# A decoder layer in split fp32: the place of one weight cast at the start and of one product at the end

## The chip, the cores and the metric

The kernel runs on one core of a Trainium2 chip. A core has a matrix engine (PE, which loads its stationary operand through PEld), a vector engine (DVE), a scalar engine (ACT), GpSimd (POOL) and SyncE (SP), which issues most of the DMAs. Every engine works through a queue of its own, in order, and waits for the others by semaphores. The metric is the device time of one execution in microseconds; lower is better. The time before is 980.24 us, the median of three runs (980.25, 978.34 and 980.24).

## What is computed

The input x has 1024 rows (positions) and 1024 columns. The reference, cut to what matters here:

```python
h = rms_norm(x, pre_g)                      # rows scaled by 1/root(mean of squares), columns by pre_g
z = jnp.einsum('bsd,de->bse', h, w_in)      # 1024 x 1024 by 1024 x 7184
qa, ka, va, ga, qb, kb, vb, gb, gk_low = split_columns(z)
oa = diff_attention(qa, ka, va, lam)        # 8 heads; then a norm and a gate silu(ga)
ob = gla_chunked(qb, kb, vb, log_a)         # 4 heads of gated linear attention; norm, gate silu(gb)
y = jnp.einsum('bse,ed->bsd', jnp.concatenate([oa, ob], axis=-1), w_out)
return x + rms_norm(y, post_g)
```

The change touches the first two lines of this and the last one. [...]

## The kernel before, in words

**The input product.** z is worked out by a scheme of seven block products instead of eight (Strassen's). h is cut into four blocks h11, h12, h21, h22 of 512 rows by 512 columns, each kept transposed, and each pair of weight column groups into four blocks b11 to b22. A list `order` of pairs (p, n) says which of the products n = 1 to 7 of which weight group p comes next; it begins (0,1), (1,1), (0,2), (1,2). Groups 0 and 1 belong together ("wide"), so they share their weights: (0,1) and (1,1) use the cast of b11, (0,2) and (1,2) that of b21. The **third product** of the title is (0,2), the first that needs b21 and h12. `prepare(i)` calls `make_weights(i)` (L278), which casts the weights of product i on ACT (L315, hi) and subtracts on DVE (L316, lo). For the first four products the cast is queued with `issue_after` behind two instructions of the last row norm: an Exp on ACT (L1481) and a `tensor_scalar` on DVE (L1482). `issue_after` orders the queue of the engine that the named instruction is on, and adds no wait.

**The beginning.** Eight tiles of x, 128 rows each, are loaded, with the first weights behind the first four. `norm_x(st)` (L486) for tiles 0 to 3 takes the sum of squares on ACT (L491), the root through `rstd` (L1477: Ln and Exp on ACT, a correction step on DVE) and scales half of the columns on DVE, the other half on POOL (L482). `first(0)` (L529) transposes the scaled tiles on PE into four PSUM banks called xT (L120), one for every 128 columns; `put` (L519) makes h_hi of each on ACT (L521) and h_lo on DVE (L522), and POOL adds the two to f1hi (L542). These four pairs are h11. Product (0,1) follows, called x in the trace; then `first(1)` does the same for h12, and (1,1) and (0,2) follow. `norm_x` of tiles 4 and 5 and of 6 and 7 (called xt in the trace) comes behind that in the program; POOL scales these whole (L482), and `blocks(j)` transposes them from 30 us on.

**What sets the order.** The program's text is no schedule: a scheduler at build time simulates the engines and fixes the order of each queue, by readiness and by the place in the text. Matmuls and transposes keep the order of the text (L116, L119). `pin` (L977) with a true first argument, and `keep_in_program_order`, fix an instruction behind the one before it in the text on the same engine. Where nothing is pinned, ACT's and DVE's orders come from the simulation.

**The end.** The output product is accumulated in PSUM for eight row tiles, in the order ENDS. `finish(n)` (L1436) does the last matmuls of tile n (called yps in the trace), squares each half of 512 columns on ACT with a running sum (L1445; its second part, ACTIVATION_READ_ACCUMULATOR, delivers the sum), takes the root with `rstd` and multiplies by post_g and the root. For the last two tiles (LAST = 2) the product with post_g is made by itself, so that only one instruction for each half (L1464, which also adds x) is left behind the root: half 0 in L1451, half 1 in L1455, which is queued behind `rstd`'s first DVE instruction, the sum for the root (L1482).

Of the kernel before, what the change touches and what calls it, by code (L numbers as in the profile page):

```python
# [10 lines left out]
AF = mybir.ActivationFunctionType  # L11
ALU = mybir.AluOpType
# [5 lines left out]
NT = S // P  # L18
KT = D // P
HB = 4  # L20
# [11 lines left out]
def hymba_kernel(  # L32
# [20 lines left out]
    nc = tc.nc  # L53
    act, dve, pool, pe, sp = nc.scalar, nc.vector, nc.gpsimd, nc.tensor, nc.sync

    def fp(t):
        return t.bitcast(F32)

    def cols(half):
        return slice(half * 512, half * 512 + 512)  # L60
# [3 lines left out]
    pre_g = const.tile([P, KT], F32, name="pre_g")  # L64
# [45 lines left out]
    def take_bank(shape, name):  # L110
        i = free.pop(0)
        return bank(i, shape, name), i
# [6 lines left out]
    def tr(dst, src):  # L119
        tc.keep_in_program_order(pe.transpose(dst, src, ident))  # L120
# [25 lines left out]
    def at(part, j):  # L146
        per = HB // len(part)
        return part[j // per][:, j % per]
# [53 lines left out]
    y, z = len(pairs) - 2, len(pairs) - 1  # L202
# [35 lines left out]
    def prepare(i):  # L238

        if i >= len(order) or i in ws:  # L240
            return
        if i < 4:

            act_ins, dve_ins = normed[0][:2]
            with tc.issue_after(act_ins.ins), tc.issue_after(dve_ins.ins):
                make_weights(i)
        else:
            make_weights(i)
# [29 lines left out]
    def make_weights(i):  # L278
        p, n = order[i]
        if wide(p) and p % 2:  # L280
            ws[i] = ws_wide[p - 1, n]
            return
        if p in early and n < 3:
            src = early[p][n - 1]
        else:
            fetch_raw(p, n, i)
            if wide(p):
                (b11, b21), (b12, b22) = ([raws[q].get(kh) for kh in range(2)] for q in (p, p + 1))
            else:
                top, bot = raws[p][0], raws[p][1]  # L290
                b11, b12 = top[:, :, :P], top[:, :, P:]
                b21, b22 = bot[:, :, :P], bot[:, :, P:]


            def sub(dst, a, b):
                dve.tensor_tensor(dst, a, b, ALU.subtract)  # L296
                return dst

            if n == 5:
                src = sub(b11, b12, b11)  # L300
            elif n == 6:
                src = sub(b11, b22, b11)
            elif n == 4:
                src = sub(b21, b21, b11)
            elif n == 7:
                src = sub(b12, b22, b12)
            else:
                src = {1: b11, 2: b21, 3: b22}[n]
        if wide(p):
            w = [ap.tile([P, HB, 256], F32R, tag="ring", name="w", bufs=NRING) for _ in range(2)]  # L310
            ws_wide[p, n] = w
        else:
            w2 = ap.tile([P, 2, HB, P], F32R, tag="ring", name="w", bufs=NRING)
            w = [w2[:, 0], w2[:, 1]]
        act.copy(w[0], src)  # L315
        dve.tensor_tensor(w[1], src, fp(w[0]), ALU.subtract)  # L316
        ws[i] = w
# [163 lines left out]
        x_cs = xs[st][:, cs]  # L481
        return engine.tensor_scalar(x_cs, x_cs, norms[st], 1.0, ALU.mult, ALU.mult)  # L482

    norms, normed = {}, []

    def norm_x(*sts):  # L486
        n = len(sts)
# [30 lines left out]

    def put(ps, k, dst, j):  # L519
        hi, lo = dst  # L520
        act.activation(at(hi, j), ps, AF.Copy, scale=pre_g[:, k : k + 1])  # L521
        dve.scalar_tensor_tensor(  # L522
            at(lo, j), ps, pre_g[:, k : k + 1], fp(at(hi, j)), ALU.mult, ALU.subtract
        )


# [2 lines left out]
    def first(h):  # L529

        ps = [take_bank([P, 512], "xT") for _ in range(HB)]
        for i in range(4):
            for j in range(HB):
                k = h * HB + j
                tr(ps[j][0][:, i * P : (i + 1) * P], xs[i][:, k * P : (k + 1) * P])
        hi, lo = H[("h11", "h12")[h]]
        for j in range(HB):
            put(ps[j][0], h * HB + j, (hi, lo), j)
            if h:
                act.activation(f1[h][:, j], ps[j][0], AF.Copy, scale=pre_g[:, h * HB + j : h * HB + j + 1])  # L540
            else:
                pool.tensor_tensor(f1[h][:, j], fp(at(hi, j)), fp(at(lo, j)), ALU.add)  # L542
            free.append(ps[j][1])

    def parts(n, j, f):
        hi, lo = block(n)
        act.copy(at(hi, j), f)
        dve.tensor_tensor(at(lo, j), f, fp(at(hi, j)), ALU.subtract)  # L548
# [46 lines left out]
    def go(n):  # L595
        for _ in range(n):
            i = made[0]
            if i == len(order):
                return
            made[0] = i + 1  # L600
            for a in range(4):
                prepare(i + a)
            step(i)
            if order[i][0] > EARLY and not (wide(order[i][0]) and order[i][0] % 2):
                wo_step(order[i][1])
            if fill and next(fill[0], 0) == 0:
                fill.pop(0)

    prepare(0)
    first(0)  # L610
    for i in range(1, 4):
        prepare(i)
    go(1)
    first(1)
    go(2)
    norm_x(4, 5)
# [360 lines left out]
    def pin(first, ins):  # L977

        if first:
            tc.keep_in_program_order(ins)  # L980
# [385 lines left out]
    parts_d, ps_d = {}, {}  # L1366
    opened.update(dict.fromkeys(Y))

    LAST, ENDS = 2, [4, 5, 6, 7, 0, 1, 2, 3]
# [12 lines left out]
    def last_times(st, dh, part, e):  # L1382
        mh, ml = part
        hi, lo = wo[e]
        for i, (a, b) in enumerate(((mh, hi), (ml, hi), (mh, lo))):
            mm(
                ps_d[st, dh], a[:, e - 4, :], b[:, cols(dh)],
                start=False, stop=(e == 7 and i == 2), skip_group_check=True,
            )
# [16 lines left out]
    post_g = fin.tile([P, D], F32, name="post_g", bufs=1)  # L1406
# [29 lines left out]
    def finish(n):  # L1436
        st = ENDS[n]
        rows = slice(st * P, (st + 1) * P)
        y = fin.tile([P, D], F32, name="y")
        ssq = const.tile([P, 4, 1], F32, tag="end_ssq", name="ssq", bufs=3)  # L1440
        for dh in range(2):
            for e in range((8, 8, 7 - 3 * dh)[n] if n < 3 else 4, 8):
                last_times(st, dh, parts_d[st], e)
            junk = fin.tile([P, 512], F32, name="junk", bufs=2)
            pin(True, act.activation(  # L1445
                junk, ps_d[st, dh], AF.Square, scale=D**-0.5, accum_out=ssq[:, 2 + dh]
            ))
            if not dh:
                dve.tensor_scalar(ssq[:, 0], ssq[:, 2], EPS, None, ALU.add)
                if n >= NT - LAST:  # L1450
                    dve.tensor_tensor(y[:, cols(0)], ps_d[st, 0], post_g[:, cols(0)], ALU.mult)  # L1451
        ins = rstd(nc, ssq, ssq[:, 3], ssq[:, 0])[2]
        if n >= NT - LAST:
            with tc.issue_after(ins.ins):
                dve.tensor_tensor(y[:, cols(1)], ps_d[st, 1], post_g[:, cols(1)], ALU.mult)  # L1455
        for dh in range(2):
            cs = cols(dh)
            if n < NT - LAST:
                dve.scalar_tensor_tensor(
                    y[:, cs], ps_d[st, dh], ssq[:, 1], post_g[:, cs], ALU.mult, ALU.mult  # L1460
                )
                pool.dma_start(out[0, rows, cs], y[:, cs], accum_op=ALU.add)
            else:
                dve.scalar_tensor_tensor(  # L1464
                    y[:, cs], y[:, cs], ssq[:, 1], xts[n][:, cs], ALU.mult, ALU.add
                )
                sp.dma_start(out[0, rows, cs], y[:, cs])
# [3 lines left out]
    for n in range(NT):  # L1471
        prime(n + 2)
        fetch(n + 4)
        finish(n)


def rstd(nc, t, s, eps, pin=None):  # L1477

    pin = pin or (lambda ins: ins)
    pin(nc.scalar.activation(t[:, 1], s, AF.Ln, bias=eps))  # L1480
    exp = pin(nc.scalar.activation(t[:, 1], t[:, 1], AF.Exp, scale=-0.5))  # L1481
    half = pin(nc.vector.tensor_scalar(t[:, 2], s, eps, -0.5, ALU.add, ALU.mult))  # L1482
    if t.shape[2] == 1:
        pin(nc.vector.scalar_tensor_tensor(
            t[:, 2], t[:, 1], t[:, 2], t[:, 1], ALU.mult, ALU.mult
        ))
    else:
        pin(nc.vector.tensor_tensor(t[:, 2], t[:, 2], t[:, 1], ALU.mult))
        pin(nc.vector.tensor_tensor(t[:, 2], t[:, 2], t[:, 1], ALU.mult))
    last = nc.vector.scalar_tensor_tensor(  # L1490
        t[:, 1], t[:, 2], 1.5, t[:, 1], ALU.add, ALU.mult
    )
    return exp, pin(last), half
# [32 lines left out]
```

## Time and profile before

| | |
|---|---|
| median of three runs | 980.24 us |
| the profiled execution's own time | 979.08 us |
| its span, first to last instruction | 977.4 us |
| time of that execution outside the span | 1.7 us |
| instructions | 15766 |
| mean clock granted to PE | 0.999 |
| PE's three longest waits after its first product | 1.3, 0.9 and 0.7 us |

A row of the timeline reads: start in us from the span's beginning, duration in us, engine, line of the kernel, operation, tile written and tiles read, shapes, and how many instructions were merged; in brackets stands how long the engine was idle before and what ended that. A row of the chain reads: start, duration, engine, tile and line. The chain is followed back from the last instruction to what released each step. Neighbouring instructions of one engine are shown to overlap by about 0.1 us, since the next begins while the last one drains; so the distance of two starts tells what an instruction costs its queue.

### The profile page before, as it was taken

How to read it: one execution, taken by the hardware profiler on the slowest of the kernel's cores; microseconds unless marked ns; L12 is line 12 of the kernel's file. 1: busy time of each engine (PE TensorE's matmuls, PEld its weight loads, DVE VectorE, ACT ScalarE, POOL GpSimd, SP SyncE). 2: the span in 40 equal slices, each digit the busy share in tenths (PEclk: the TensorE clock that was granted, in tenths of full speed). 3: DMA queues.
4: the chain of work that ended last, by engine and by line, in shares of the span. 5: the costliest groups of instructions: out<-in, count | busy, mean ns of one | idle time of the engine just before them, and what ended most of it. 6: DMA issues, size and time to landing. Idle time of an engine off the chain costs nothing.

```text
span 977.4 us, 15766 instructions
## 1 busy us (share of the span) xinstructions
PE 956.7 (98%) x5338; PEld 830.4 (85%) x5338; DVE 735.4 (75%) x1452; ACT 600.5 (61%) x1164; POOL 142.9 (15%) x158
## 2 busy tenths in 40 slices
PE   5999999999999999999999999999999999999997
PEld 5998988888889998999888888878888888888785
DVE  6887597789866667686786876487888888898554
ACT  8742455487357455454665775366776687887773
POOL 4300000000000010000200002121322222443321
PEclk9999999999999999999999999999999999999999
DMA  9432446656774868897987866987656669994677
GB/s 345 151 110 91 139 135 205 231 179 225 238 247 162 264 187 286 254 294 229 293 259 243 273 202 191 407 269 272 197 186 228 240 199 344 340 294 105 151 208 147
DMA packets 152593, 220.45 MB, mean 226 GB/s; under 512 B 17104, under 2 KB 83664, under 8 KB 152416
## 3 DMA queue, kind: packets, MB, share of 16 engines
q1 hardware_dynamic: 146176, 203.71, 64.1%
q0 software_dynamic: 6336, 15.73, 7.0%
q8 instruction: 42, 0.69, 0.3%
q14 instruction: 39, 0.32, 0.1%
HBM read 133.93 MB, written 88.60 MB: 228 GB/s over the span
## 4 chain that ended last, share of the span: by engine, by line
PE 95%; DVE 2%; ACT 1%; DMA 1%; issue 1%; POOL 0%; SPq 0%; DVEq 0%; ACTq 0%; POOLq 0%
PE x L117 24%; PE y L117 15%; PE z L117 15%; PE ypart L117 13%; PE sc L117 7%; PE po L117 5%; PE yps L117 4%; PE wtr L120 3%; PE gpo L117 3%; PE kv L117 1%; PE gkl_ps L117 1%; PE pa L117 1%; DMA x<-in_x_dram 1%; PE xT L120 1%; DVE s_lo L548 0%
## 5 line engine op out<-in xcount | busy, mean ns | idle before, releaser
L315 ACT CAST w<-w_raw 128x512 fp32r<-128x512 f32 (+1 forms) x164 | 112.4, 688 | 94.7 <-PE y L117 44.1
L316 DVE TENSOR_TENSOR w<-w_raw,w 128x512 fp32r<-128x512 f32 (+1 forms) x164 | 126.7, 774 | 50.1 <-ACT w L315 43.3
L1049 ACT ACTIVATE p<-p,stt 128x896 f32<-128x896 f32 (+7 forms) x128 | 99.3, 777 | 36.7 <-DVE stt L1039 33.9
L427 ACT COPY s<-x 128x512 f32<-128x512 f32 x84 | 49.1, 585 | 84.4 <-PE x L117 84.3
L775 POOL TENSOR_SCALAR_AFFINE_SELECT gan<-gan 128x512 f32<-128x512 f32 x8 | 16.5, 2060 | 485.4 <-ACT gan L774 449.8
L296 DVE TENSOR_TENSOR w_raw<-w_raw 128x512 f32<-128x512 f32 (+1 forms) x96 | 75.9, 791 | 13.9 <-DMA w_raw<-in_w_in_dram 12.6
L1039 DVE CUSTOM_DVE_ANT_0 p<-sc,maskt 128x512 f32<-128x512 f32 (+3 forms) x128 | 74.3, 585 | 14.5 <-PE sc L117 13.3
L117 PE MATMUL ypart<-wo_hi,m_hi 128*128 128x512 f32 x192 | 79.5, 414 | 0.1
L117 PE MATMUL y<-h_hi,w 128*128 128x512 f32 x320 | 79.6, 391 | 0.0
L117 PE MATMUL z<-s_hi,w 128*128 128x512 f32 x320 | 79.6, 391 | 0.0
L117 PE MATMUL x<-s_hi,w 128*128 128x512 f32 x320 | 79.6, 391 | 0.0
L1055 POOL TENSOR_SCALAR p<-p,stt,lam 128x1024 f32<-128x1024 f32 (+3 forms) x64 | 56.2, 879 | 146.9 <-DVE stt L1054 141.9
L117 PE MATMUL ypart<-wo_hi,m_lo 128*128 128x512 f32 x192 | 75.5, 393 | 0.0
L117 PE MATMUL ypart<-wo_lo,m_hi 128*128 128x512 f32 x192 | 75.4, 393 | 0.0
L117 PE MATMUL sc<-k,q 128*128 128x512 f32 (+1 forms) x192 | 69.0, 363 | 1.3 <-DVE stt L1039 1.2
L117 PEld LDWEIGHTS x<-s_hi,w 128*128 128x128 f32 x320 | 59.7, 188 | 12.2
L117 PEld LDWEIGHTS y<-h_hi,w 128*128 128x128 f32 x320 | 59.6, 188 | 12.2
L117 PEld LDWEIGHTS z<-s_hi,w 128*128 128x128 f32 x320 | 59.5, 188 | 12.0
L117 PE MATMUL sc<-ks,q 128*128 128x512 f32 (+1 forms) x192 | 66.1, 347 | 0.0
L1097 ACT CAST wt_hi<-wtr 128x512 fp32r<-128x512 f32 (+1 forms) x80 | 42.7, 534 | 24.6 <-PE wtr L120 23.8
L1098 DVE TENSOR_TENSOR wt_lo<-wtr,wt_hi 128x512 fp32r<-128x512 f32 (+1 forms) x80 | 50.7, 633 | 8.6 <-ACT wt_hi L1097 8.0
L1058 DVE SCALAR_TENSOR_TENSOR p<-p,stt,p 128x1024 f32<-128x1024 f32 (+3 forms) x64 | 52.1, 814 | 4.1 <-POOL p L1055 3.9
(226 smaller groups left out, 2247.7 us busy)
## 6 DMA issues: line engine op xcount, KB each, us to landing
w_raw<-in_w_in_dram SPq DMA_DIRECT2D x56, 512.0 KB, 4.7
wo_raw<-in_w_out_dram SPq DMA_DIRECT2D x32, 256.0 KB, 3.0
wo_d<-wo_hi SPq DMA_DIRECT2D x32, 256.0 KB, 2.8
wo_d<-wo_raw SPq DMA_DIRECT2D x32, 256.0 KB, 3.8
q<-q_d SPq DMA_DIRECT2D x32, 256.0 KB, 4.7
k<-k_d SPq DMA_DIRECT2D x32, 256.0 KB, 5.7
ks<-k_d SPq DMA_DIRECT2D x64, 128.0 KB, 6.2
v<-v_d SPq DMA_DIRECT2D x16, 512.0 KB, 7.0
```

What stands on the lines that cost most here:

```text
L117: tc.keep_in_program_order(pe.matmul(*a, **k))
L120: tc.keep_in_program_order(pe.transpose(dst, src, ident))
L296: dve.tensor_tensor(dst, a, b, ALU.subtract)
L315: act.copy(w[0], src)
L316: dve.tensor_tensor(w[1], src, fp(w[0]), ALU.subtract)
L427: act.copy(b[k], ps)
L1039: ins = dve.tensor_tensor_reduce(p[:, a:e], sc[:, : e - a], maskt[:, NZ + P - (e - a) :] if last else maskt[:, : e - a], 1.0, 3e38 if i == ...
L1049: act.activation(p[:, :n], p[:, :n], AF.Exp, bias=st[:, m : m + 1], scale=-1.0, accum_out=st[:, 2 + m : 3 + m],)
L1055: pool.tensor_scalar(p1[:, :n], p1[:, :n], st[:, 5:6], lam, ALU.mult, ALU.mult)
L1058: dve.scalar_tensor_tensor(p0[:, :n], p0[:, :n], st[:, 4:5], p1[:, :n], ALU.mult, ALU.subtract)
L1097: act.copy(hi[:, :n], pt[:, :n])
L1098: dve.tensor_tensor(lo[:, :n], pt[:, :n], fp(hi[:, :n]), ALU.subtract)
```

## The change

It has two parts that do not touch each other.

1. `first` returns the ACT and DVE instructions of its last `put`, and those of `first(0)` are kept in `firsts`. `prepare(1)` to `prepare(3)`, which come behind `first(0)` in the text, queue their weight casts behind these two in place of the norm's two. Of these only `prepare(2)` issues anything: one cast on ACT and one subtraction on DVE of 128x1024 (the odd products (1,1) and (1,2) take over the weights of (0,1) and (0,2)). `prepare(0)` runs while `firsts` is empty and stays where it was. No DMA is issued in it, since both halves of the raw weights are asked for ahead.
2. For the last tile alone (n = 7) the product of half 1 with post_g is pinned behind the earlier DVE instruction of the text, that is ahead of `rstd`, and `rstd`'s five instructions are pinned behind it in the text's order. Tile n = 6 keeps its order.

```diff
-            act_ins, dve_ins = normed[0][:2]
+            act_ins, dve_ins = firsts or normed[0][:2]
             with tc.issue_after(act_ins.ins), tc.issue_after(dve_ins.ins):
                 make_weights(i)
...
-        act.activation(at(hi, j), ps, AF.Copy, scale=pre_g[:, k : k + 1])
-        dve.scalar_tensor_tensor(
-            at(lo, j), ps, pre_g[:, k : k + 1], fp(at(hi, j)), ALU.mult, ALU.subtract
+        return act.activation(at(hi, j), ps, AF.Copy, scale=pre_g[:, k : k + 1]), (
+            dve.scalar_tensor_tensor(
+                at(lo, j), ps, pre_g[:, k : k + 1], fp(at(hi, j)), ALU.mult, ALU.subtract
+            )
         )
...
-            put(ps[j][0], h * HB + j, (hi, lo), j)
+            last = put(ps[j][0], h * HB + j, (hi, lo), j)
...
+        return last
...
     prepare(0)
-    first(0)
+    firsts += first(0)
     for i in range(1, 4):
         prepare(i)
...
-        ins = rstd(nc, ssq, ssq[:, 3], ssq[:, 0])[2]
-        if n >= NT - LAST:
+        if n == NT - 1:
+            pin(True, dve.tensor_tensor(y[:, cols(1)], ps_d[st, 1], post_g[:, cols(1)], ALU.mult))
+        ins = rstd(nc, ssq, ssq[:, 3], ssq[:, 0], lambda ins: pin(n == NT - 1, ins) or ins)[2]
+        if NT - LAST <= n < NT - 1:
             with tc.issue_after(ins.ins):
                 dve.tensor_tensor(y[:, cols(1)], ps_d[st, 1], post_g[:, cols(1)], ALU.mult)
```

More of the change, by code (lines that the diff above doesn't have):

```diff
@@ L482, in scale_x @@
         return engine.tensor_scalar(x_cs, x_cs, norms[st], 1.0, ALU.mult, ALU.mult)
-    norms, normed = {}, []
+    norms, normed, firsts = {}, [], []
     def norm_x(*sts):
```

## The prediction

> **What bounds the kernel now.** I read the page's busy shares and its chain first, then the waits of PE from the first product on, then the chain of the first 60 us in order of time, and last the timeline at the two places of the change.
>
> ```profile
> PE 956.7 (98%) x5338; PEld 830.4 (85%) x5338; DVE 735.4 (75%) x1452; ACT 600.5 (61%) x1164; POOL 142.9 (15%) x158
> ...
> PE 95%; DVE 2%; ACT 1%; DMA 1%; issue 1%; POOL 0%; SPq 0%; DVEq 0%; ACTq 0%; POOLq 0%
> ```
>
> PE is busy for 956.7 of 977.4 us and is 95% of the chain that ends last. What is not PE's is 20.7 us: mostly the beginning, the end, and these waits (us in total, times, longest):
>
> ```profile
> PE y L117 <- DVE s L565: 1.3, 1, 1.3
> ...
> PE y L117 <- ACT s L427: 0.7, 1, 0.7
> PE x L117 <- ACT h_hi L521: 0.6, 1, 0.6
> ```
>
> The 0.6 us for h_hi is the place of the first edit. The chain around it:
>
> ```profile
> 12.17 0.50 DVE x L482
> ...
> 12.71 0.91 PE xT L120 x3
> ...
> 13.68 0.69 ACT h_hi L521
> ...
> 14.41 5.76 PE x L117 x24
> 20.17 1.75 PE xT L120 x16
> ...
> 30.55 0.87 PE xT L120 x8
> ...
> 41.83 0.69 DVE gv_st L403
> ...
> 59.37 0.74 PE x L117 x4
> ```
>
> The scaled x is transposed, ACT makes the first h_hi, and PE starts its first product at 14.41. From there to 41.83 the chain is PE; from 41.83 to 59.37 it is DVE, started by PE's result; after that PE again. So what PE gains at 14.41 reaches the end only if nothing else is late at one of the hand-overs.
>
> **The first edit: what it frees.** ACT and PE around the first h_hi:
>
> ```profile
> 11.60 1.03 ACT L315 CAST w<-w_raw 128x1024 fp32r<-128x1024 f32 x1
> ...
> 12.72 1.05 ACT L315 CAST w<-w_raw 128x1024 fp32r<-128x1024 f32 x1
> ```
>
> ```profile
> 12.71 0.47 PE L120 MATMUL xT<-ident,x 128*128 128x128 f32 x1 [0.49 <-DVE x L482]
> ```
>
> The cast at 12.72 is the third product's. It holds ACT to 13.77, and h_hi starts at 13.68, in its tail. The bank that the first h_hi reads got its last transpose at 12.71 + 0.47 = 13.18. With the cast gone from there h_hi can start at about 13.18 + 0.05 (the hand-over from h_hi's end, 14.37, to PE, 14.41, is 0.04) = 13.23: 0.45 us earlier, and PE's first matmul at 13.96. Nothing but this cast stood between.
>
> How much of the 0.45 us is left when PE goes on depends on PE's pace, which changes in this stretch:
>
> ```profile
> 16.53 1.91 PE L117 MATMUL x<-w,h_hi 128*128 128x256 f32 x8
> ```
>
> ```profile
> 26.55 1.12 PE L117 MATMUL y<-w,h_lo 128*128 128x256 f32 x8
> ```
>
> Eight equal matmuls take 1.91 us early and 1.12 us later, though the page gives the granted clock as 9 tenths or more in every slice. A start-to-start step is (1.91 - 0.41) / 7 = 0.21 early, with 0.41 an estimate of one slow matmul's length, and (1.12 - 0.28) / 7 = 0.12 later. If the changeover moves along with the start, all 0.45 us is kept. If it stays at its time, the 0.45 us holds two slow steps, which take 2 x 0.12 = 0.24 us off the fast part. No row decides; I take the middle, 0.35 us, with both ends kept.
>
> [...]
>
> **What it adds and moves.** One cast (1.05 us, a step of about 0.96 from 12.72 to 13.68) goes behind the fourth h_hi on ACT, one subtraction behind the fourth h_lo on DVE. No DMA is issued with them, so SP's and POOL's queues are passed by none. Their product is the third, whose weights PE does not need before 24.6 us. What stands behind them:
>
> ```profile
> 15.97 1.07 ACT L491 ACTIVATE junk<-xt 128x1024 f32<-128x1024 f32 x1
> ...
> 21.62 2.42 ACT L521 ACTIVATE h_hi<-xT,pre_g 128x512 fp32r<-128x512 f32 x4 [0.21 <-PE xT L120]
> ```
>
> ```profile
> 14.21 1.21 DVE L316 TENSOR_TENSOR w<-w_raw,w 128x1024 fp32r<-128x1024 f32 x1
> 25.64 0.74 DVE L522 SCALAR_TENSOR_TENSOR h_lo<-xT,pre_g,h_hi 128x512 fp32r<-128x512 f32 x1
> ```
>
> ```profile
> 28.69 1.14 POOL L482 TENSOR_SCALAR xt<-xt,ssq 128x1024 f32<-128x1024 f32 x1
> ```
>
> ```profile
> 30.15 0.40 PE L117 MATMUL y<-w,h_lo 128*128 128x256 f32 x2
> 30.39 0.82 PE L120 MATMUL xT<-ident,xt 128*128 128x128 f32 x6
> ```
>
> ACT: the h_hi start 0.45 earlier, then comes the cast of 0.96, so the squares of the later tiles (L491 from 15.97) start about 0.5 later. Before the h_hi of h12 ACT idled 0.21, so these come 0.3 us later, the last at 24.04 + 0.3 = 24.34. The third product, at 24.6 - 0.35 = 24.3, reads the fourth of them six matmuls, 0.7 us, after its start: hidden, with 0.6 us to spare.
>
> DVE: the subtraction at 14.21 stood ahead of all h_lo, so the h_lo come about 1.1 us earlier, and it itself afterwards. Nobody waits for these h_lo on the path: PE reads the first at 18.45 by its own pace (16.53 and 1.91 us of matmuls more). But POOL's four sums f1hi start earlier with them, and DVE and POOL get in each other's way:
>
> ```profile
> 16.17 1.29 POOL L542 TENSOR_TENSOR f1hi<-h_hi,h_lo 128x512 f32<-128x512 f32 x1 [2.95 <-DVE h_lo L522]
> ```
>
> ```profile
> 19.91 2.26 POOL L542 TENSOR_TENSOR f1hi<-h_hi,h_lo 128x512 f32<-128x512 f32 x1
> ```
>
> ```profile
> 19.14 1.88 DVE L296 TENSOR_TENSOR w_raw<-w_raw 128x1024 f32<-128x1024 f32 x1 [0.42 <-DMA w_raw<-in_w_in_dram]
> ```
>
> ```profile
> 20.95 1.24 DVE L1482 TENSOR_SCALAR ssq<-ssq,eps_t 128x2 f32<-128x2 f32 x1
> ```
>
> ```profile
> 22.17 1.21 DVE L296 TENSOR_TENSOR w_raw<-w_raw 128x1024 f32<-128x1024 f32 x1
> ```
>
> The same DVE operation takes 1.21 us when POOL is idle and 1.88 beside f1hi; f1hi takes 1.29 alone and 2.26 beside it; a tiny operation of 0.2 us takes 1.24. The subtraction moves into this stretch. I take it that it uses the slot that the earlier h_lo freed, and that DVE and POOL are where they were by 22.2: cost nothing. The other end is one wait each, 0.67 + 0.97 = 1.64 us later on POOL. POOL's scaling of xt ends at 28.69 + 1.14 = 29.83, and PE wants it at 30.39: a cover of 0.56 us, of which an earlier PE uses 0.35. So at the bad end PE waits 1.64 - 0.56 = 1.1 us more than before. The last h_lo of h12 ends at 26.38 and is read at 26.55 + 6 x 0.12 = 27.3, which covers 0.9 us.
>
> At 41.83 DVE had been idle for 0.16 us only. What it does before follows the transposes at 30.39 and their successors, so it moves along; if it did not, 0.16 us would be all that is kept. I keep 0.35.
>
> **The second edit.** The last instructions:
>
> ```profile
> 970.72 0.60 ACT L1445 ACTIVATE junk<-yps 128x512 f32<-128x512 f32 x1 [2.03 <-PE yps L117]
> 971.22 0.19 ACT L1445 ACTIVATION_READ_ACCUMULATOR junk<-yps 128x1 f32 x1
> 971.44 0.29 ACT L1480 ACTIVATE ssq<-ssq 128x1 f32<-128x1 f32 x1
> 971.77 0.20 ACT L1481 ACTIVATE ssq<-ssq 128x1 f32<-128x1 f32 x1
> ```
>
> ```profile
> 968.80 0.69 DVE L1451 TENSOR_TENSOR y<-yps,post_g 128x512 f32<-128x512 f32 x1
> 971.45 0.21 DVE L1482 TENSOR_SCALAR ssq<-ssq 128x1 f32<-128x1 f32 x1 [1.95 <-ACT junk L1445]
> 971.57 0.68 DVE L1455 TENSOR_TENSOR y<-yps,post_g 128x512 f32<-128x512 f32 x1
> 972.17 0.21 DVE L1484 SCALAR_TENSOR_TENSOR ssq<-ssq 128x1 f32<-128x1 f32 x1
> ```
>
> ACT squares the bank from 970.72 to 971.41. Then DVE does the sum (a step of 0.12) and the product (a step of 0.60), and L1484 starts at 972.17, though the Exp that it needs ended at 971.97: the product costs about 0.17 on the path. Swapped, there are two ways. If the product runs beside the square, from 970.73 to 971.41, the sum starts at 971.45 as before and L1484 at 972.00: 0.17 gained. If it starts only when the square has read the bank, it runs from 971.45; the sum starts at 972.05, and L1484, which needs the sum, at 972.05 + 0.21 + 0.04 = 972.30: 0.13 lost. The nearest row is L1451, the same product on the other half, at 968.80: it too stands behind ACT's reading of its bank, though another instruction is ahead of it there. I take +0.13, with -0.17 as the other end. Behind the product on DVE stand the root, L1464 and the two output DMAs, all on the path, so either end counts in full.
>
> [...] No row here shows two engines reading one bank at once, nor that they may not.
>
> **Sum.** -0.35 + 0.13 = -0.22 us: 979.08 - 0.22 = 978.86 for the profiled execution, and 980.24 - 0.22 = 980.02 for the median, which lies 1.2 us above it. The forecast's own range is 980.24 - 0.45 - 0.17 = 979.6 to 980.24 + 0.5 = 980.7. A measurement of this kernel tells about 0.2%, 1.96 us, from no change, so faster means under 978.28 and slower over 982.20.
>
> **The rivals.**
>
> The first casts do not come earlier. The chain puts three transposes, not one, ahead of h_hi; they end at 12.71 + 0.91 = 13.62. Were h_hi waiting for the third, it would start at 13.67, where it starts now. Against it: ACT was busy to 13.77 anyway, and a first bank needs its own transposes only. It gives 980.24 + 0.13 = 980.4.
>
> POOL is late at 30.39 (the slower side). The moved subtraction waits for one f1hi (0.67), makes the next wait (0.97), and the root's first operation L1482 of the later tiles then waits for a whole f1hi (1.24 - 0.21 = 1.03). The later roots, and with them POOL's scaling of xt, come 2.67 us later. It decides from 0.56 us on, the cover at 30.39; PE then waits 2.67 - 0.56 = 2.1 us more, with 0.13 at the end: 982.5. For it speaks that each of these waits is in the rows; against it that f1hi also starts 1.1 us earlier, so the pile-up may be over earlier.
>
> The queues are ordered anew by the build's scheduler, and PE's waits of 1.3 (L565) and 0.7 us (L427) close: 980.24 - 0.35 - 2.0 + 0.13 = 978.0. For it: both hang on one instruction's place in DVE's and ACT's queues. Against it: the chain from 41.83 to 59.37 is DVE, end to end, so closing the first wait only brings PE to DVE's next result sooner.
>
> **How the numbers follow.** Forecast 0.47, no earlier casts 0.15, POOL late 0.20, closed waits 0.18. The forecast and the first rival are within 0.2%: 0.62; faster 0.18; slower 0.20. The likeliest gives 980.0. The range reaches from the third rival, 978.0, to the second, 982.5, and what lies past either end is left out.
>
> **What would show it.** In the changed profile: one cast ahead of h_hi and one behind the fourth, h_hi at 13.23 and the first matmul at 13.96; the first transposes of xt at about 30.04, with no wait of PE on POOL; PE's wait for L565 still about 1.3 us; at the end L1455 ahead of L1482, at 971.45 or 970.73 relative to a square at 970.72. A first h_hi later than 13.4, a wait of PE at 30 us, or new waits past 60 us would make the prediction wrong.

## The result

The changed kernel takes 981.55 us (median of 15 executions, 980.37 to 984.86), the kernel before 979.65 (15 executions on the same chip, 978.34 to 981.47). The ratio is 1.0021 with a 95% interval of 1.0014 to 1.0028: **slower by 2.0 us**, where the forecast was 0.2 faster and no change that a measurement can tell. Ratios here compare all executions of two kernels, so they can differ a little from the quotient of the medians; differences in us follow the ratio unless they name two times.

The profile after is of an execution of 984.86 us, the longest of the fifteen; its span is 983.1 us. The page's busy shares first:

```profile
PE 959.3 (98%) x5338; PEld 831.8 (85%) x5338; DVE 735.9 (75%) x1452; ACT 600.7 (61%) x1164; POOL 143.2 (15%) x158
```

As many instructions on PE as before (x5338), and 2.6 us more of busy time (956.7 before). Shares say nothing of the place. PE's waits do (total us, times, longest):

```profile
PE xT L120 <- POOL xt L482: 1.9, 2, 1.1
```

This line is new. The prediction said that there would be no such wait at 30 us. The 0.6 us for h_hi is gone, as it said. (h_hi is the cast of h to fp32r, h_lo the rest, h minus h_hi; a product is the sum of hi·hi, lo·hi and hi·lo.) The timeline of the changed kernel around the first product, with the scaling of x that releases it:

```profile
11.43 0.49 DVE L482 TENSOR_SCALAR x<-x,ssq 128x512 f32<-128x512 f32 x1
...
12.48 1.85 ACT L521 ACTIVATE h_hi<-xT,pre_g 128x512 fp32r<-128x512 f32 x3 [0.60 <-PE xT L120]
...
13.22 4.24 PE L117 MATMUL x<-w,h_hi 128*128 128x256 f32 x16
```

In this execution x was scaled 0.74 us earlier than in that of before (11.43 against 12.17), for the data landed earlier (ACT's square of the third tile starts at 7.65 in the trace after, and at 8.38 in that of before, where ACT had waited 0.63 us for the tile's DMA); so places are compared here by their distance from that row. h_hi stands 1.05 us behind it, before 1.51; the first matmul 1.79, before 2.24. **The 0.45 us of the first edit is there to the hundredth.** It is lost 17 us later:

```profile
28.93 0.38 PE L120 MATMUL xT<-ident,xt 128*128 128x128 f32 x2
30.42 0.33 PE L120 MATMUL xT<-ident,xt 128*128 128x128 f32 x1 [1.12 <-POOL xt L482]
31.52 1.25 PE L120 MATMUL xT<-ident,xt 128*128 128x128 f32 x5 [0.77 <-POOL xt L482]
32.42 3.32 PE L117 MATMUL x<-w,h_hi 128*128 128x256 f32 x16
```

PE comes to the transposes of xt 17.50 us behind the scaling of x (before 18.22), waits 1.12 and 0.77 us for POOL, and its next product starts 20.99 us behind it (before 31.18 - 12.17 = 19.01). And that product is slow: 16 matmuls take 3.32 us. A view of stretches shows why; its columns are the stretch, its length, the busy time of PE, PEld, DVE, ACT and POOL, PE's granted clock, the DMA share and GB/s:

```profile
28.00:31.00 3.00, 1.63 (x13) 1.21 (x11) 1.84 (x2) 0.05 (x1) 3.00 (x3) 1.00 1.02 307
31.00:32.00 1.00, 0.48 (x3) 0.49 (x4) 0.00 (x0) 0.04 (x1) 1.00 (x3) 0.82 0.57 133
32.00:33.00 1.00, 1.00 (x7) 1.00 (x5) 0.00 (x0) 0.83 (x2) 0.44 (x2) 0.50 0.81 172
...
35.00:36.00 1.00, 1.00 (x10) 1.00 (x10) 0.95 (x2) 0.60 (x1) 0.00 (x0) 0.97 0.44 153
```

From about 31.6 to 35.1 PE was granted half its clock (0.50). So the waits cost more than their 1.9 us here.

Why was POOL late? It is not that it had more to do. The same four scalings, before and after:

```profile
24.42 5.41 POOL L482 TENSOR_SCALAR xt<-xt,ssq 128x1024 f32<-128x1024 f32 x4 [2.25 <-ACT h_hi L521]
```

```profile
24.98 6.48 POOL L482 TENSOR_SCALAR xt<-xt,ssq 128x1024 f32<-128x1024 f32 x4 [4.70 <-ACT f1lo L541]
```

Together they start 13.55 us behind x (before 12.25) and end at 20.03 (before 17.66). POOL had been idle for 4.70 us: it waited for the root of tiles 4 and 5. DVE's queue shows what stood ahead of that root. First the rows of before that belong to it and were not shown:

```profile
22.10 0.15 DVE L1488 TENSOR_TENSOR ssq<-ssq 128x2 f32<-128x2 f32 x1
...
23.45 0.74 DVE L522 SCALAR_TENSOR_TENSOR h_lo<-xT,pre_g,h_hi 128x512 fp32r<-128x512 f32 x1
24.11 0.14 DVE L1490 SCALAR_TENSOR_TENSOR ssq<-ssq 128x2 f32<-128x2 f32 x1
```

```profile
16.10 1.80 DVE L316 TENSOR_TENSOR w<-w_raw,w 128x1024 fp32r<-128x1024 f32 x1
17.96 1.11 DVE L1486 TENSOR_SCALAR ssq<-ssq,eps_t 128x2 f32<-128x2 f32 x1
19.04 2.33 DVE L296 TENSOR_TENSOR w_raw<-w_raw 128x1024 f32<-128x1024 f32 x1
...
21.43 1.21 DVE L296 TENSOR_TENSOR w_raw<-w_raw 128x1024 f32<-128x1024 f32 x1
22.56 0.15 DVE L1492 TENSOR_TENSOR ssq<-ssq 128x2 f32<-128x2 f32 x1
22.63 0.74 DVE L522 SCALAR_TENSOR_TENSOR h_lo<-xT,pre_g,h_hi 128x512 fp32r<-128x512 f32 x1
23.30 0.14 DVE L1493 TENSOR_TENSOR ssq<-ssq 128x2 f32<-128x2 f32 x1
23.36 1.40 DVE L522 SCALAR_TENSOR_TENSOR h_lo<-xT,pre_g,h_hi 128x512 fp32r<-128x512 f32 x2
24.68 0.14 DVE L1494 SCALAR_TENSOR_TENSOR ssq<-ssq 128x2 f32<-128x2 f32 x1
```

L1492, L1493 and L1494 are the last three steps of the root (L1488, L1489 and L1490 before). Before, the first of them stood ahead of the second weight difference L296 (22.10 and 22.17), and one h_lo stood ahead of the last step. After, the first stands behind that difference and three h_lo stand ahead of the last step. The diff names none of these instructions. The build's scheduler, given one subtraction and one cast at another place, ordered their neighbours anew: on ACT too, where the copy of s now stands ahead of the Exp of tiles 4 and 5 (20.07 and 20.54; before 20.41 and 20.31). POOL's and PE's queues are as before.

At the end of the program the order is as announced:

```profile
976.29 0.60 ACT L1447 ACTIVATE junk<-yps 128x512 f32<-128x512 f32 x1 [2.03 <-PE yps L117]
...
977.01 0.69 DVE L1455 TENSOR_TENSOR y<-yps,post_g 128x512 f32<-128x512 f32 x1 [1.95 <-ACT junk L1447]
977.62 0.20 DVE L1486 TENSOR_SCALAR ssq<-ssq 128x1 f32<-128x1 f32 x1
977.93 0.22 DVE L1488 SCALAR_TENSOR_TENSOR ssq<-ssq 128x1 f32<-128x1 f32 x1
```

From the square's start to the root's second step (L1488 here, L1484 before) it takes 1.64 us; before, 972.17 - 970.72 = 1.45. The second edit costs 0.19 us.

### The profile page after: what moved, and what is told of

It reads as the page before. It is cut to its first block, busy times and chain, and to the rows that moved or that the text cites. A ratio compares the mean times of both kernels' runs of the same rounds, so it can differ in the third digit from the quotient of the medians.

```text
span 983.1 us, 15764 instructions
## 1 busy us (share of the span) xinstructions
PE 959.3 (98%) x5338; PEld 831.8 (85%) x5338; DVE 735.9 (75%) x1452; ACT 600.7 (61%) x1164; POOL 143.2 (15%) x158
## 4 chain that ended last, share of the span: by engine, by line
PE 86%; DVE 4%; DMA 4%; ACT 2%; issue 2%; SPq 1%; POOL 1%; DVEq 0%; ACTq 0%; POOLq 0%
PE x L117 21%; PE y L117 14%; PE z L117 14%; PE ypart L117 12%; PE sc L117 6%; PE po L117 5%; PE yps L117 4%; PE wtr L120 3%; PE gpo L117 2%; PE kv L117 1%; PE gkl_ps L117 1%; DMA mixd<-gate 1%; DMA w_raw<-in_w_in_dram 1%; DMA v_d<-c 1%; DVE w L316 1%
## 5 line engine op out<-in xcount | busy, mean ns | idle before, releaser
L316 DVE TENSOR_TENSOR w<-w_raw,w 128x512 fp32r<-128x512 f32 (+1 forms) x164 | 127.4, 779 | 49.6 <-ACT w L315 43.0
L296 DVE TENSOR_TENSOR w_raw<-w_raw 128x512 f32<-128x512 f32 (+1 forms) x96 | 76.4, 796 | 15.0 <-DMA w_raw<-in_w_in_dram 13.6
L117 PE MATMUL x<-s_hi,w 128*128 128x512 f32 x320 | 79.7, 391 | 0.0
L117 PE MATMUL y<-h_hi,w 128*128 128x512 f32 x320 | 79.6, 391 | 0.0
L117 PE MATMUL ypart<-wo_hi,m_hi 128*128 128x512 f32 x192 | 79.5, 414 | 0.1
L117 PE MATMUL z<-s_hi,w 128*128 128x512 f32 x320 | 79.6, 391 | 0.0
L117 PE MATMUL ypart<-wo_hi,m_lo 128*128 128x512 f32 x192 | 75.5, 393 | 0.0
L117 PE MATMUL ypart<-wo_lo,m_hi 128*128 128x512 f32 x192 | 75.4, 393 | 0.0
L117 PE MATMUL sc<-k,q 128*128 128x512 f32 (+1 forms) x192 | 69.1, 363 | 1.6 <-DVE stt L1041 1.6
L117 PEld LDWEIGHTS x<-s_hi,w 128*128 128x128 f32 x320 | 59.6, 188 | 12.6 <-ACT s L427 0.4
L117 PEld LDWEIGHTS y<-h_hi,w 128*128 128x128 f32 x320 | 59.6, 188 | 12.2
L117 PEld LDWEIGHTS z<-s_hi,w 128*128 128x128 f32 x320 | 59.5, 188 | 12.0
L117 PE MATMUL sc<-ks,q 128*128 128x512 f32 (+1 forms) x192 | 66.0, 347 | 0.0
```

The lines of the kernel that those rows point to most:

```text
L117: tc.keep_in_program_order(pe.matmul(*a, **k))
```

## The experiments

**Theory:** the order of DVE's queue between 20 and 27 us makes POOL late, and PE waits for POOL. **Rivals:** the loss comes from the end; or the moved subtraction itself, beside POOL's f1hi, makes POOL late in whatever order; or a wait of PE at 30 us is made good at the later hand-overs to DVE.

Four kernels first, on one chip. The first edit alone (the lines of `finish` as before):

> The first edit alone; the end is as in the kernel before. Theory (order): the build queues the third subtraction, the two differences and the roots of the later tiles in another order, the last root step for tiles 4 and 5 comes 1.3 us later relative to x, POOL's scaling of xt with it, and PE waits about 1.9 us for it at 30 us. Then this kernel is 1.5 to 2.0 us slower than before, with the two waits on POOL in its profile. Rival (the end): the first edit gains its 0.35 us and the loss comes from the second edit; then this kernel is 0.35 us faster than before.

Measured: 981.61 us against 979.79, ratio 1.0017 (1.0008 to 1.0026), 1.7 us slower. PE's waits of this kernel, and the place:

```profile
PE xT L120 <- POOL xt L482: 1.7, 1, 1.7
```

```profile
31.52 0.77 PE L120 MATMUL xT<-ident,xt 128*128 128x128 f32 x5 [1.71 <-POOL xt L482]
32.04 2.15 PE L117 MATMUL x<-w,h_hi 128*128 128x256 f32 x16
```

The loss lies in the first edit. PE's clock stayed at 1.00 in this execution (16 matmuls in 2.15 us), so the half clock does not follow every such wait.

The second edit alone (`prepare` and `first` as before):

> The second edit alone; the start is as in the kernel before. Theory (order): from the square's start to L1484's counterpart 1.64 us instead of 1.45, so 0.2 us slower than before, within 0.2%, and no wait of PE on POOL at 30 us. Rival (the end): 1.5 us slower or more.

Measured: 980.52 against 979.79, ratio 1.0003 (0.9994 to 1.0013). The end:

```profile
971.86 0.60 ACT L1445 ACTIVATE junk<-yps 128x512 f32<-128x512 f32 x1 [2.03 <-PE yps L117]
972.35 0.19 ACT L1445 ACTIVATION_READ_ACCUMULATOR junk<-yps 128x1 f32 x1
...
972.58 0.69 DVE L1453 TENSOR_TENSOR y<-yps,post_g 128x512 f32<-128x512 f32 x1 [1.95 <-ACT junk L1445]
...
973.50 0.22 DVE L1486 SCALAR_TENSOR_TENSOR ssq<-ssq 128x1 f32<-128x1 f32 x1
```

973.50 - 971.86 = 1.64 us again. The product starts when ACT's second part has ended, at 972.35 + 0.19 = 972.54. DVE idles 1.95 us before it; of these, 972.58 - 971.86 = 0.72 us are ACT's reading of the bank, and the rest is the wait for PE's last matmuls, which ACT waits for too. The rival of the end is out.

The first edit with before's order of the rest, but for one step (below). `hold` counts the instructions of each kind as they come in the text, from 0 (hi and lo 4 to 7 are those of `first(1)`; root 0 to 5 are Ln, Exp and the four DVE steps of tiles 4 and 5, 6 to 11 those of tiles 6 and 7; sub are the differences of L296, snap the copies of s) and queues one behind another, with no wait. The two `norm_x` are moved up in the text, since an edge can name earlier text only:

```diff
     for i in range(1, 4):
         prepare(i)
+    norm_x(4, 5)
+    norm_x(6, 7)
     go(1)
...
-    norm_x(4, 5)
-    norm_x(6, 7)
...
+    RULES = {('hi', 4): [('root', 7)], ('hi', 5): [('root', 7)], ('hi', 6): [('root', 7)],
+             ('hi', 7): [('root', 7)], ('snap', 0): [('root', 1)], ('sub', 1): [('root', 3)],
+             ('lo', 4): [('root', 9)], ('lo', 5): [('root', 5), ('root', 10), ('lo', 4)],
+             ('lo', 6): [('lo', 5)], ('lo', 7): [('root', 11), ('lo', 6)]}
+    def hold(kind, ins):
+        n = len(kept[kind])
+        kept[kind].append(ins)
+        for other, m in RULES.get((kind, n), ()):
+            tc.add_manual_dep(
+                ins.ins, kept[other][m].ins.name,
+                mybir.DependencyInfo(mybir.DependencyClass.NoSync, mybir.DependencyReason.DATA),
+                reason="order by hand",
+            )
+        return ins
```

> The first edit alone, and the other instructions of ACT and DVE up to 30 us held in the order of the kernel before by ordering edges that wait for nothing: Exp ahead of the copy of s and of h_hi, the root steps ahead of h_lo. Theory (order): POOL's scaling of xt is no later than before relative to x, PE does not wait for it, and the first matmul's 0.45 us is kept: 0.3 to 0.7 us faster than before. Rival (the moved work itself): the subtraction's new place beside POOL's f1hi costs POOL its 1.3 us whatever the order of the rest: 1 us slower or more, with PE's waits on POOL still there.

Measured: 980.07 against 979.79, ratio 1.0000 (0.9990 to 1.0009). DVE and POOL in this kernel (L1519 and L1521 are the first product and the last step of the root; x was scaled at 11.44):

```profile
16.11 1.79 DVE L316 TENSOR_TENSOR w<-w_raw,w 128x1024 fp32r<-128x1024 f32 x1
...
21.30 0.15 DVE L1519 TENSOR_TENSOR ssq<-ssq 128x2 f32<-128x2 f32 x1
21.37 1.21 DVE L296 TENSOR_TENSOR w_raw<-w_raw 128x1024 f32<-128x1024 f32 x1
...
23.31 0.14 DVE L1521 SCALAR_TENSOR_TENSOR ssq<-ssq 128x2 f32<-128x2 f32 x1
...
24.11 0.64 DVE L1521 SCALAR_TENSOR_TENSOR ssq<-ssq 128x2 f32<-128x2 f32 x1
24.67 1.40 DVE L548 SCALAR_TENSOR_TENSOR h_lo<-xT,pre_g,h_hi 128x512 fp32r<-128x512 f32 x2
```

```profile
23.61 5.41 POOL L506 TENSOR_SCALAR xt<-xt,ssq 128x1024 f32<-128x1024 f32 x4 [2.25 <-ACT h_hi L547]
```

```profile
25.11 1.51 PE L117 MATMUL y<-w,h_lo 128*128 128x256 f32 x8
```

POOL's scalings stand 12.17 to 17.58 us behind x; before, 12.25 to 17.66. PE did not wait for POOL. The moved subtraction took 1.79 us beside f1hi, and yet the second difference ended 11.14 us behind x (before 11.21): the work itself does not make POOL late. That rival is out, and the loss of 1.7 us is gone.

The gain of 0.3 to 0.7 us that the theory named is not there either, and the trace shows why. The held order differs from before's in one step: the last root step of tiles 6 and 7 (L1521 at 24.11) stands ahead of the third h_lo, where before it stood behind it (L1490, 25.57). Beside a scaling on POOL it takes 0.64 us, and the last h_lo ends 26.07 - 11.44 = 14.63 us behind x (before 26.38 - 12.17 = 14.21). PE, which comes early, waits for it: eight matmuls of h_lo take 1.51 us, where 1.12 is usual, so 0.39 us is lost.

The opposite: the kernel before with the changed kernel's order, by the same `hold`; the two `norm_x` stay where they are in the text, and rest counts the subtractions of L316.

```diff
+    RULES = {('root', 1): [('snap', 0)], ('root', 3): [('lo', 3)], ('root', 4): [('lo', 4)],
+             ('root', 5): [('lo', 6)], ('root', 7): [('hi', 6)], ('root', 10): [('lo', 7)],
+             ('root', 11): [('rest', 2)], ('lo', 5): [('lo', 4)], ('lo', 6): [('lo', 5)],
+             ('lo', 7): [('lo', 6)], ('hi', 5): [('hi', 4)], ('hi', 6): [('hi', 5)],
+             ('hi', 7): [('hi', 6)]}
```

> The kernel before, with nothing of the change, and its Exp, root steps, copies and h_hi/h_lo held in the order that the changed kernel has there (one step, the first root product, stands one place further ahead). Theory (order): POOL's scaling of xt starts about 1.3 us later, PE waits for it at 30 us by about 1.3 - 0.56 = 0.7 us, or 1.7 with one more scaling stretched by DVE: 0.7 to 1.8 us slower than before. Rival (the moved work itself): as before, within 0.3 us, with no wait on POOL.

Measured: 981.42 against 979.79, ratio 1.0011 (1.0001 to 1.0020), 1.1 us slower with nothing of the change in it. Its POOL and PE (x at 11.45):

```profile
24.93 5.47 POOL L506 TENSOR_SCALAR xt<-xt,ssq 128x1024 f32<-128x1024 f32 x4 [3.50 <-ACT w L315]
...
30.04 1.18 PE L120 MATMUL xT<-ident,xt 128*128 128x128 f32 x8
```

POOL starts 13.48 and ends 18.95 us behind x, 1.2 and 1.3 us later than before. In the profiled execution, the fastest of the twelve (979.12 us), PE was 0.4 us late itself (18.59), because its pace changed late, and so it waited too shortly to be listed; the expected 0.7 us of wait is not in this trace. By the measured times the order alone costs something, at the lower end of what was expected, with an interval that just clears 1.

Four more, on one chip. The whole change, mended with edges on ACT alone (`hold` and the place of the two `norm_x` as in the run with before's order); DVE's queue then comes out as in the kernel above that holds all:

```diff
+    RULES = {('hi', 4): [('root', 7)], ('hi', 5): [('root', 7)], ('hi', 6): [('root', 7)],
+             ('hi', 7): [('root', 7)], ('snap', 0): [('root', 1)]}
```

> The whole changed kernel, with ordering edges on ACT alone in the first 30 us: Exp ahead of the copy of s and of h_hi, as in the kernel before; DVE's queue then comes out as there too. Theory (order): PE's waits on POOL at 30 us are gone, the start gains 0.3 us and the end loses 0.2, so within 0.5 us of the kernel before and 1.5 us or more faster than the changed kernel. Rival (the two edits hurt each other, or something past 60 us): still 1.5 us slower than before.

Measured: 979.45 against 979.99, ratio 0.9994 (0.9985 to 1.0002). The mended change lies between 1.5 us faster than the kernel before and 0.2 slower; its interval lies clear of the changed kernel's (1.0014 to 1.0028, each against the kernel before on its own chip). POOL's scalings stand 12.18 us behind x (11.54):

```profile
23.72 5.39 POOL L506 TENSOR_SCALAR xt<-xt,ssq 128x1024 f32<-128x1024 f32 x4 [2.26 <-ACT h_hi L547]
```

The last h_lo ends 14.63 us behind x here too, and holds PE as in the kernel above.

A test of the step from POOL to PE, with no queue's order changed:

```diff
                 scale_x(st, slice(0, D))
+                if st == 4:
+                    pool.tensor_scalar(xs[4], xs[4], 1.0, 1.0, ALU.mult, ALU.mult)
```

> The kernel before with all queues as they are, and on POOL one operation more behind the second scaling of xt: tile 4 multiplied by 1, 1.1 us alone or 2.1 beside DVE. It tries the step from POOL to PE without any order changed. Theory: POOL's scaling ends 1.1 to 2.1 us later, the cover in this kernel is 0.56 us, so PE waits 0.6 to 1.5 us at 30 us and the kernel is 0.6 to 1.5 us slower, more if PE then falls back to its slow pace. Rival (PE's wait there is made good at the later hand-overs to DVE): a wait on POOL at 30 us, and the time as before within 0.3 us.

Measured: 980.57 against 979.99, ratio 1.0003 (0.9995 to 1.0012). POOL ended 18.68 us behind x, 1.0 later than before, but PE came to the transposes at 18.62 (0.4 later than in the trace of before, with its pace changing late) and did not wait. This run tells nothing: the dose was as small as PE's own spread.

The first edit with DVE's edges alone, else in the same way:

```diff
+    RULES = {('sub', 1): [('root', 3)], ('lo', 4): [('root', 9)],
+             ('lo', 5): [('root', 5), ('root', 10), ('lo', 4)], ('lo', 6): [('lo', 5)],
+             ('lo', 7): [('root', 11), ('lo', 6)]}
```

> The first edit alone, ACT's queue as the changed kernel has it, DVE's root steps held ahead of the h_lo (the first root product still behind the second difference). Theory (order, and DVE's part of it decides): the last root step for tiles 4 and 5 comes straight behind that difference, 1.2 us earlier than in the first edit alone; POOL is in time or at most 0.5 us late; within 0.6 us of the kernel before. Rival (ACT's copy ahead of the first Exp decides): as the first edit alone, 1.5 to 2.0 us slower, with 1.7 us of waits on POOL.

Measured: 979.85 against 979.99, ratio 0.9994 (0.9984 to 1.0004), POOL's scalings 11.69 to 17.60 us behind x (11.70), no wait of PE on POOL. The last two of the four:

```profile
26.12 3.19 POOL L506 TENSOR_SCALAR xt<-xt,ssq 128x1024 f32<-128x1024 f32 x2 [0.52 <-ACT f1lo L570]
```

ACT still had the copy of s ahead of Exp (20.34 and 20.81). So it is DVE's order that decides, and ACT's only through what the scheduler makes of it for DVE.

Another way to free the root: the two differences behind it.

```diff
-                dve.tensor_tensor(dst, a, b, ALU.subtract)
-                return dst
+                behind = tc.issue_after(normed[0][1].ins) if i < 14 else nullcontext()
+                with behind:
+                    dve.tensor_tensor(dst, a, b, ALU.subtract)
+                return dst
```

> The first edit alone, with the two early weight differences of DVE queued behind the last root step; ACT's queue as in the changed kernel. Theory (order): the roots of tiles 4 and 5 no longer stand behind two differences of 1.2 us, POOL's scaling starts 1 us or more ahead of where the first edit alone has it, PE does not wait for POOL, and the kernel is 0 to 0.7 us faster than before. Rival (the differences are needed early): a new wait of PE for their weights past 32 us takes the gain, 0.5 us slower than before or more.

Measured: 981.28 against 979.99, ratio 1.0011 (1.0003 to 1.0020), 1.1 us slower: a miss. No wait past 32 us is new, so the rival is not it either. POOL and PE:

```profile
21.60 2.23 POOL L484 TENSOR_SCALAR xt<-xt,ssq 128x1024 f32<-128x1024 f32 x2 [1.22 <-ACT ssq L1484]
25.99 5.09 POOL L484 TENSOR_SCALAR xt<-xt,ssq 128x1024 f32<-128x1024 f32 x2 [2.16 <-ACT f1lo L543]
...
31.13 0.77 PE L120 MATMUL xT<-ident,xt 128*128 128x128 f32 x5 [1.11 <-POOL xt L484]
```

Tiles 4 and 5 come 3.35 us earlier than in the first edit alone, as meant. But the root of tiles 6 and 7 still ends only at 25.83, and the differences, moved beside the last two scalings, stretch these to 5.09 us, where two take 2.23 undisturbed. POOL ends 19.55 us behind x, and PE waits 1.11 us. What counts is POOL's last scaling, and the cure brought back the lateness there.

Last, POOL late by a larger, known amount, in the kernel that holds before's order, and beside it that kernel again as its control:

```diff
                 scale_x(st, slice(0, D))
+                if st == 4:
+                    pool.tensor_scalar(xs[4], xs[4], 1.0, 1.0, ALU.mult, ALU.mult)
+                    pool.tensor_scalar(xs[4][:, :512], xs[4][:, :512], 1.0, 1.0, ALU.mult, ALU.mult)
```

> The first edit with the order of the kernel before held, and on POOL two operations more behind the four scalings of xt: tile 4 multiplied by 1, once whole (1.1 us) and once in half (an estimated 0.6). PE's first transpose at 30 us reads tile 4, so it waits for both. This makes POOL late by a known amount and changes no order before 60 us. Theory: POOL ends 1.7 us later, PE waits 1.4 us for it, and the kernel is 1.2 to 2.0 us slower than the same kernel without the two operations. Rival (a wait of PE there is made good at the later hand-overs): the wait is there and the time is the same within 0.4 us.

> The first edit with the order of the kernel before held, as measured above, beside the kernel with the two POOL operations, as its control on the same chip. Theory: no wait of PE on POOL, 0.3 us faster than the kernel before by the start, so a ratio between 0.999 and 1.0005.

Measured: the control 979.90 against 980.02, ratio 0.9996 (0.9987 to 1.0005); with the two operations 983.10, ratio 1.0032 (1.0021 to 1.0043), so 3.1 us slower than before and 983.10 - 979.90 = 3.2 slower than the control, more than the 1.2 to 2.0 that were expected.

```profile
29.09 2.02 POOL L531 TENSOR_SCALAR xt<-xt 128x1024 f32<-128x1024 f32 x1
31.19 0.62 POOL L532 TENSOR_SCALAR xt<-xt 128x512 f32<-128x512 f32 x1
...
31.86 1.62 PE L120 MATMUL xT<-ident,xt 128*128 128x128 f32 x8 [2.26 <-POOL xt L532]
```

```profile
32.00:33.00 1.00, 1.00 (x7) 1.00 (x7) 0.00 (x0) 0.34 (x1) 0.79 (x3) 0.64 0.86 242
33.00:34.00 1.00, 1.00 (x7) 1.00 (x6) 0.00 (x0) 0.83 (x2) 0.00 (x0) 0.50 1.08 355
34.00:35.00 1.00, 1.00 (x7) 1.00 (x7) 0.76 (x2) 0.20 (x1) 0.00 (x0) 0.50 0.77 263
35.00:36.00 1.00, 1.00 (x7) 1.00 (x7) 0.65 (x1) 0.32 (x1) 0.00 (x0) 0.66 0.11 37
```

POOL's first extra operation met DVE and took 2.02 us, so the wait was 2.26 us where 1.4 was expected, and in this execution the half clock came on top. Nothing of it is made good later: the last rival is out.

All profiled executions side by side, in us behind the start of DVE's last scaling of x: PE's first matmul; its first matmul (L117) at full pace; the end of POOL's last operation on xt; PE's arrival at the transposes of xt; the product behind them; and PE's matmul behind its wait for the copy of s at some 70 us, past the stretch in which the chain runs through DVE. The last column is the measured ratio to before.

| kernel | first | full pace | POOL ends | transposes | product | at 70 us | ratio |
|---|---|---|---|---|---|---|---|
| before | 2.24 | 7.71 | 17.66 | 18.22 | 19.01 | 58.70 | 1 |
| changed | 1.79 | 6.64 | 20.03 | 17.50 | 20.99 | 61.85 | 1.0021 |
| first edit alone | 1.80 | 7.09 | 19.85 | 17.70 | 20.42 | 60.10 | 1.0017 |
| second edit alone | 2.29 | 6.73 | 17.66 | 17.84 | 18.63 | 58.32 | 1.0003 |
| first edit, before's order | 1.79 | 6.66 | 17.58 | 17.90 | 18.69 | 58.37 | 1.0000 |
| the same, as control | 1.80 | 6.86 | 17.57 | 17.90 | 18.69 | 58.38 | 0.9996 |
| before, changed order | 2.23 | 10.07 | 18.95 | 18.59 | 19.53 | 59.21 | 1.0011 |
| changed, mended on ACT | 1.79 | 5.35 | 17.56 | 17.91 | 18.70 | 58.38 | 0.9994 |
| first edit, DVE's edges | 1.79 | 9.39 | 17.60 | 18.20 | 18.99 | 58.69 | 0.9994 |
| first edit, differences late | 1.79 | 9.50 | 19.55 | 18.00 | 20.12 | 59.82 | 1.0011 |
| before, one POOL operation more | 2.29 | 10.11 | 18.68 | 18.62 | 19.41 | 59.09 | 1.0003 |
| before's order, POOL late | 1.79 | 7.10 | 20.26 | 20.31 | 21.58 | 62.42 | 1.0032 |

The column at 70 us differs from that of the product by 39.68 to 39.70 us in all kernels but the two whose PE fell to half clock (40.86 and 40.84): what is won or lost at 30 us comes through to 70 us unchanged. In the four kernels with full pace behind 9 us the pace changed earlier than the column says, at some 7.5 to 8.5 us, where sixteen transposes of x stand between two products. This is an estimate from the rows: the matmuls of h_lo ahead of the transposes still step by some 0.21 us (eight in 1.91 us in two of the four kernels, eight in 1.85 and seven in 1.70 in the others), and eight of h_lo behind them take 1.12.

## Where the prediction was right and where it failed

- **The earlier h_hi: right.** 0.45 us at the first matmul in every kernel with the first edit.
- **What PE keeps of it: plausible up to the transposes, not shown behind them.** Forecast 0.24 to 0.45, taken 0.35. The two executions whose pace changes at nearly the same place can be compared: PE comes to the transposes 17.50 us behind x in the changed kernel (full pace at 6.64) and 17.84 with the second edit alone (6.73), 0.34 earlier. The place of that change varies from 5.35 to some 8.5 us, and PE's arrival without the first edit from 17.84 to 18.62, so one execution of each cannot show a term of this size. And no kernel carries the gain to the product at 30 us. Where POOL is late, the wait takes it. Where the order was held, the product comes at 18.69 or 18.70 us in all three executions, though their pace changes at 5.35, 6.66 and 6.86: it is set by the last h_lo. That is 0.3 us earlier than in the profile of before, but the second edit alone, with nothing of the first, has it at 18.63. The prediction counted 0.9 us of cover for that h_lo and did not set an earlier PE and a later h_lo against it together.
- **The moved subtraction costs nothing, DVE back in place by 22.2: right for the work.** With the order held the second difference and POOL's scalings end within 0.1 us of before. The last h_lo ends 0.4 us later; the root step beside POOL explains it, and no run parts that from the moved subtraction.
- **Readings of the pace and the range.** 1.91 to 1.12 us is a factor of 1.7, and the steps, 0.21 and 0.12 us, are one of 1.8. The 0.5 us at the upper end of the forecast's own range has no row behind it.
- **The step that failed** is the sentence that DVE *and POOL* are where they were by 22.2. The prediction moved two instructions within queues that it took as fixed, and looked at what stands behind them in time. But the order of these queues is a result of the build, and it changed: the root of tiles 4 and 5 fell behind a difference and two more h_lo, POOL started 1.3 us later, and one more scaling met a DVE operation. So a term that was put at nothing cost 1.7 us. POOL's end moved by 2.37 us in the changed kernel against the rival's 2.67, and the cover of 0.56 was the right one to look at.
- **The rivals.** "The first casts do not come earlier" is out with the 0.45 us. "POOL is late at 30.39" had the place, the cover and nearly the size (PE 2.1 us later by the forecast; in the traces waits of 1.9 and 1.7, and the product 1.98 and 1.41 later), but not the cause: it had the root held up by f1hi, which the runs with the order held show to be over in time. "The queues are ordered anew" had the cause with the wrong sign: it looked for waits that close, and not for a wait that opens. PE's 1.3 us for s (L567 now) and 0.7 us for the copy of s are unchanged in all kernels.
- **The second edit: the right side.** +0.13 forecast, +0.19 measured; the hand-over from L1484 to L1486 in the run with the second edit alone takes 0.11 us (973.39 to 973.50) where 0.04 was counted. In that trace DVE's product starts 0.72 us behind the start of ACT's square (971.86 and 972.58), when ACT's second part has ended (972.54). No row shows the two on the bank at once, which the other end of the forecast, -0.17, needs.
- **Not foreseen:** that a wait of PE can cost more than its length, by 1.2 us in the product behind it (3.32 us in the changed kernel, 2.15 in the first edit alone).

The sum of what the runs show: 1.7 us from the first edit, 0.2 from the second, 2.0 measured. How often the half clock is part of it is not settled: of the profiled executions of the changed kernel and of the first edit alone, one has it. The mean clocks point at a minority: 4 of the 15 executions of the changed kernel ran at 0.996 or 0.997 (982.36 to 984.86 us), the others at 0.998 or 0.999, and the median of those eleven, 981.04, is still 1.4 us above the kernel before. It is a hint only, since the execution with POOL late has the stretch at a mean of 0.998.

## What to carry to other kernels

Where a scheduler at build time fixes the queues, moving one instruction can reorder its neighbours: compare the queues of both builds, row by row, ahead of any sum, and look for small steps (here a root of 128x2) that feed another engine. A cover between two engines, here 0.56 us, is the budget for any such reordering; when one is used up, pin the small producer ahead of the large work instead of accepting the order that comes out. And a cure is judged by the last hand-over that it moves, not the first: one cure here brought the last scaling late, and another, which brought POOL back in time, let PE run into the last h_lo.

## What the runs showed of the hardware

- **Half clock after a short wait.** A wait of 2.26 us (POOL late), and two of 1.12 and 0.77 us with one transpose between them (the changed kernel), were followed by a stretch at clock 0.50; a wait of 1.71 us (the first edit alone) and one of 1.11 us (differences late) were not: there the views show 1.00 from 28 to 40 us. Added up the waits are 2.26 and 1.89 against 1.71 and 1.11; four executions do not show what decides. PE's step in the slow stretch is 0.21 us (33.00 and 33.21 in the trace of the changed kernel), as at the start of the kernel (16.74 and 16.95 in that of before), where the views show the clock as 1.00: the granted clock of these profiles does not show the slow start. The stretches last about 3.4 us: from the rows above, (1 - 0.64) / 0.5 = 0.72, 2 and 0.68 us with POOL late, and (1 - 0.82) / 0.5 = 0.36, 3 and 0.06 us in the changed kernel.
- **DVE and POOL beside each other.** POOL's scaling takes 1.1 us alone (1.14 at 28.69 in the trace of before) and 2.0 to 2.2 beside one DVE operation of 1.2 us (2.16 at 26.08 in that of the changed kernel, beside L316); DVE's difference of 1.21 us takes 2.33 beside f1hi, and a root step of 128x2 takes 1.11 there and 0.22 alone. In these rows the one's time is at most about the sum of both: 2.16 against 1.14 + 1.21, 2.33 against 1.21 + 1.29 and 1.11 against 0.22 + 1.29, where 1.29 is f1hi at 16.17 in the trace of before, beside h_lo.
- **Waits that come and go.** PE waits past 360 us, for c (L411) and gu (L805 in the changed kernel), are in some executions and not in others, whatever the kernel: 0.8 and 1.0 us in that of the changed kernel, 0.2 and 1.4 with the second edit alone, none in that of before. They add up to 1.8 us, so spans of two executions do not tell edits of this size apart.
